# Gate stage: norm rows loaded step by step and transposes half a block later; the indexer's keys share two blocks of 328 columns with the values

## The chip, the cores and the metric

The kernel runs on one core of a Trainium2 chip. The metric is the device time of one execution in microseconds (us), the median of three runs. TensorE is called PE, VectorE DVE, ScalarE ACT, GpSimd POOL, and SyncE SP, as the profile does.

## The reference, cut to what matters

The program is a decoder trunk of two layers on 256 tokens of 2048 features, all in float32. The two stages that the change touches are the gated embedding at the end of each layer and the first half of the sparse-attention mixer of layer 1.

```
x = layer_norm(ALPHA * x + conv_glu(x)) * g + b
x = x + sigmoid(x @ ple_w_gate[i]) * (p[i] @ ple_w_proj[i])          # "gate stage"

q, k, v, qi, ki, wi = split(x @ dsa_w_in)      # 2048, 512, 512, 16*128, 128, 16 columns
ki = layer_norm(ki)                            # keys of the indexer
score[t, s] = sum_h wi[t, h] * relu(qi[t, h] . ki[s])    # 16 index heads
keep the 64 best s <= t for each t
o[h] = softmax(q[h] . k / sqrt(128) + bias[h, t - s]) @ v      # over the kept s, 16 heads
```

## The kernel before, in words

Every float32 weight is split into a high and a low part: a block of weights is loaded into a `raw` tile by a DMA that SP issues (L105), ACT writes `hi` (L109), DVE writes `lo` (L110), and PE multiplies both. `raw`, `hi` and `lo` have three buffers each, so a load can start when DVE has finished the `lo` of three blocks ago. Tokens are split likewise: `xT` holds the transposed x as a high and a low part.

There are two forms of matmul loop, both Python generators that hand over one step at a time. `gemm_t_steps` (L128, L132) holds the weights still and moves the tokens: 256 output columns at a time, 4 steps of 16 matmuls. `gemm_steps` (L154, L155, L158) holds the tokens still and moves n weight columns: per block of 128 features three matmuls for each half `a` of the tokens, so 96 matmuls over 16 blocks. With n = 512 a step covers 2 blocks of features (8 steps of 12 matmuls), with n = 144 it covers 4 (4 steps of 24). In the last step the two halves are finished one after the other, and `done(a, ps)` is called for each.

**Gate stage** (`ple`, both layers): four column blocks of 512. The first two run their first three steps by turns; then `affine` is called for four column slices: two row DMAs on POOL's queue (L205, one buffer each) and four DVE operations (L299, L300). Then the rest of the two blocks by turns, then blocks 2 and 3. `done` computes the sigmoid on ACT (L739), two DVE operations (L740, L741), and, in layer 0 only, transposes the new x with four PE transposes (`t_ps`, L199) into the `xT` of the next mixer (ACT L192, DVE L193).

**Sparse attention** (`dsa`, layer 1): the 144 columns of `ki` and `wi` run by turns with the first 256 columns of `qi`. `keys` normalizes each half with a chain of small DVE operations and transposes it on PE (`ki_ps`, L800). `index` computes one head's score (`sc_ps`, L813; ACT Relu L815; DVE L818 or L820). The other 14 heads follow (`scores`), and while the first eight are at hand POOL's queue gets eight loads of `bias` (L831). Then DVE finds the kept positions (L842, L843) and POOL adds the mask to `bias` (L848), while PE computes the keys `kT` and then the values `v` (512 columns). `attend` follows, two heads for every 256 columns of q: `lg_ps` L863, DVE L865 reads `bias`, and so on.

The order on each engine is fixed when the program is built: a scheduler takes the instructions in program order, moves an instruction ahead where it deems it ready earlier by its own estimates, and puts `hi` and `lo` 1000 places ahead (`W_AHEAD`). At run time each engine works through its list in order.

Of the kernel before, what the change touches and what calls it, by code (L numbers as in the profile page):

```python
# [16 lines left out]
P = 128  # L17
S = 256
D = 2048
KT = D // P  # L20
D_FF = 5120
ALPHA = 4.0 ** 0.25
LN_EPS = 1e-5
# [3 lines left out]
NR = 383  # L27
# [37 lines left out]
class Trunk:  # L65
# [30 lines left out]
                               reason="order")  # L96


    def weights(self, src, rows, nk, cols):

        nc = self.nc
        c0, n = cols
        shape = [P, nk, n]
        raw = self.wp.tile(shape, F32, tag="raw", name="raw")
        nc.sync.dma_start(out=raw, in_=src[rows:rows + nk * P, c0:c0 + n].rearrange("(k p) n -> p k n", p=P))  # L105
        hi = self.hl.tile(shape, F32R, tag="hi", name="hi")
        lo = self.hl.tile(shape, F32R, tag="lo", name="lo")
        with self.tc.high_priority(offset=W_AHEAD):
            nc.scalar.activation(hi, raw, AF.Copy)  # L109
            ins = nc.vector.tensor_tensor(lo, raw, hi.bitcast(F32), op=ALU.subtract)  # L110
        if self.behind:
            self.after(ins, self.behind.pop())
        return hi, lo
# [23 lines left out]
                done((c - c0 + o) // P, q[:m, :])  # L137
            yield

    def gemm_steps(self, src, c0, n, x, kt, done):  # L140


        nc = self.nc
        ps = [self.mm.tile([P, 512], F32, tag="mm", name="b_ps") for _ in range(2)]
        nk = min(1 << (1024 // n).bit_length() - 1, kt)
        for k0 in range(0, kt, nk):
            m = min(nk, kt - k0)
            hi, lo = self.weights(src, k0 * P, m, (c0, n))

            for halves in (range(2),) if k0 + m < kt else ((0,), (1,)):  # L150
                for k in range(m):
                    for a in halves:
                        xh, xl = (x(k0 + k)[:, j, a * P:(a + 1) * P] for j in range(2))
                        nc.tensor.matmul(ps[a][:, :n], xh, hi[:, k, :], start=k0 + k == 0, stop=False)  # L154
                        nc.tensor.matmul(ps[a][:, :n], xl, hi[:, k, :], start=False, stop=False)  # L155
                for k in range(m):
                    for a in halves:
                        self.last = nc.tensor.matmul(ps[a][:, :n], x(k0 + k)[:, 0, a * P:(a + 1) * P], lo[:, k, :],  # L158
                                                     start=False, stop=k0 + k == kt - 1)
                if k0 + m == kt:  # L160
                    done(a, ps[a][:, :n])
            yield
# [91 lines left out]
    def layer_norm(self, pool, st, g, b, gb, copies):  # L254


        nc, x, xT = self.nc, self.x, self.xT
        with self.tc.high_priority():
            mv = pool.tile([P, 2, 2], F32, tag="lmv", name="lmv")
# [35 lines left out]
        def affine(pool, nb, start):  # L295
            cs = slice(nb * 512, (nb + 1) * 512)
            gr, br = (self.rows(pool, r[cs], 512, k, 1, start) for r, k in ((g, "lng"), (b, "lnb")))
            for a in range(2):
                nc.vector.tensor_tensor(x[:, a, cs], x[:, a, cs], gr, op=ALU.mult)  # L299
                nc.vector.tensor_tensor(x[:, a, cs], x[:, a, cs], br, op=ALU.add)  # L300

        return affine

# [357 lines left out]
    def ffn(self, i, affine):  # L661
        nc, tc, t = self.nc, self.tc, self.t
        with tc.tile_pool(name="hp", bufs=1) as hp, tc.tile_pool(name="fp", bufs=1) as pool:
# [25 lines left out]
            for n in range(0, NF, 2):  # L689
                steps = (self.gemm_t_steps(t["ffn_w_gate"][i], n * P, 256, self.xT, lambda m, ps: gate(n + m, ps)),  # L690
                         self.gemm_t_steps(t["ffn_w_up"][i], n * P, 256, self.xT, lambda m, ps: up(n + m, ps)))
                if n:
                    for x in steps:
                        self.go_(x)
                else:
                    self.go_(*steps)
                if n % 4 == 0:
                    next(distances, None)
                if n in (6, 14, 22, 30):
                    affine(pool, n // 8, self.mark)  # L700
            return self.project(pool, t["ffn_w_down"][i], hT, NF, t["ln2_g"][i], t["ln2_b"][i], lambda: self.fill)


# [25 lines left out]
        return fill  # L729

    def ple(self, i, affine, xT=None, out=None):
        nc, tc, t, x = self.nc, self.tc, self.t, self.x
        with tc.tile_pool(name="pp", bufs=1) as pool:
            def done(nb):
                cs = slice(nb * 512, (nb + 1) * 512)

                def f(a, ps):
                    s = pool.tile([P, 512], F32, tag="sg", name="sg", bufs=2)
                    nc.scalar.activation(s, ps, AF.Sigmoid)  # L739
                    nc.vector.tensor_tensor(s, s, self.pw[:, a, cs], op=ALU.mult)  # L740
                    nc.vector.tensor_tensor(x[:, a, cs], x[:, a, cs], s, op=ALU.add)  # L741
                    if out is not None:
                        nc.sync.dma_start(out=out[0, a * P:(a + 1) * P, cs], in_=x[:, a, cs])
                    if xT is not None:
                        self.to_xT(xT, x[:, a, cs], a, nb * 4)
# [12 lines left out]


    def distances(self, pool):  # L760
# [21 lines left out]
    def dsa(self, pool, xT, oT):  # L782
        nc, tc, t = self.nc, self.tc, self.t
        w_in = t["dsa_w_in"]
        span = (P, S)
# [4 lines left out]
        ki = pool.tile([P, 2, P], F32, tag="ki", name="ki")  # L790
        pt = self.sp.tile([P, 2, P], F32, tag="sp", name="ki_ps")

        def keys(a, ps):
            nc.vector.tensor_scalar(wi[:, a], ps[:, P:], 1.0 / (4.0 * math.sqrt(128.0)), None, op0=ALU.mult)
            st = pool.tile([P, 6], F32, tag="kst", name="kst", bufs=2)
            nc.vector.bn_stats(st, ps[:, :P])
            mu, r = self.moments(pool, st, LN_EPS)
            nc.vector.scalar_tensor_tensor(ki[:, a], ps[:, :P], mu, g, op0=ALU.subtract, op1=ALU.mult)
            nc.vector.scalar_tensor_tensor(ki[:, a], ki[:, a], r, b, op0=ALU.mult, op1=ALU.add)
            nc.tensor.transpose(pt[:, a], ki[:, a], self.ident)  # L800
            if a:
                nc.vector.tensor_copy(kiT, pt.rearrange("p a s -> p (a s)"))


        sc = [pool.tile([P, span[a]], F32, tag=f"sc{a}", name=f"sc{a}") for a in range(2)]

        def index(h, ps):
            qi = pool.tile([P, S], F32, tag="qi", name="qi", bufs=2)
            self.fold(pool, qi, ps)
            p2 = self.sp.tile([P, 3 * P], F32, tag="sp", name="sc_ps")  # L810
# [4 lines left out]
            nc.scalar.activation(rl, p2, AF.Relu)  # L815
# [11 lines left out]
        def scores(n, ps):  # L827
            index(n + 2, ps)
            if n < 8:
                a, h = n // 4, n % 4 * 4  # L830
                nc.gpsimd.dma_start(out=bias[a][:, h:h + 4],  # L831
                                    in_=bass.AP(tensor=fx.tensor, offset=fx.offset + 255 - P * a + NR * h,
                                                ap=[[R, P], [NR, 4], [1, span[a]]]))

        self.gemm_t(w_in, 3328, 1792, xT, scores)

        for a in range(2):
# [48 lines left out]
    def run(self, out):  # L886
# [19 lines left out]
        self.ple(0, affine, xT=xT)  # L906
        pp.release()
        with tc.tile_pool(name="da", bufs=1) as pool:
            self.dsa(pool, xT, aT)
# [36 lines left out]
```

## Time and the profile before

| | us |
|---|---|
| median of three runs | 2877.74 |
| the three runs | 2878.88, 2877.74, 2874.36 |
| the profiled execution | 2870.2 |
| its span in the trace | 2868.4 |

The trace is that of the profiled execution, which was 7.5 us shorter than the median; 1.8 us of its time lie outside the span. All times of single instructions are on the span's clock. In the gate stage of layer 0 PE works from about 1611 to 1707 us, in the first half of the sparse attention from 1707 to 1873 us, and in the gate stage of layer 1 from about 2771 to 2863 us.

### The profile page before, as it was taken

What the parts mean: (1) busy time and instruction counts of PE and PEld (TensorE: products, weight loads), DVE (VectorE), ACT (ScalarE), POOL (GpSimd) and SP (SyncE); (2) the same over time, 40 slices, a digit from 0 to 9 for tenths busy, and PEclk for the clock granted to TensorE, in tenths of its full rate; (3) what the DMA queues carried; (4) which work ended last, traced back from release to release, by engine and by line L of the source; (5) the groups of instructions that cost most, each with busy time, mean ns of one, the idle gap of its engine ahead of it and who ended that gap; (6) DMA issues with size and microseconds to landing.
All of it is one profiled execution on the core that took longest, in us unless ns stands there. A gap on an engine that the chain in (4) does not pass through costs nothing.

```text
span 2868.4 us, 40302 instructions
## 1 busy us (share of the span) xinstructions
PE 2816.9 (98%) x15022; PEld 2406.3 (84%) x15022; DVE 1883.4 (66%) x3256; ACT 1401.6 (49%) x2147; POOL 311.8 (11%) x580
## 2 busy tenths in 40 slices
PE   8999999999999999999999999999999999999999
PEld 6788888888787888888888888888888888888887
DVE  6878877778655666666554755766576666654565
ACT  4455555555334655555433544455365555543354
POOL 0143234540000000000000000210000000000000
PEclk9999999999999999999999999999999999999999
DMA  6655556655465566666656566554656666656555
GB/s 195 174 154 152 162 158 164 173 151 144 140 221 176 185 201 202 200 204 205 194 194 192 191 190 182 173 157 138 195 167 196 194 191 197 198 191 191 191 190 191
DMA packets 409620, 520.90 MB, mean 182 GB/s; under 512 B 28268, under 2 KB 296944, under 8 KB 409168
## 3 DMA queue, kind: packets, MB, share of 16 engines
q1 hardware_dynamic: 402192, 499.91, 57.4%
q0 software_dynamic: 7232, 18.42, 2.6%
q8 instruction: 118, 1.93, 0.3%
q14 instruction: 78, 0.64, 0.1%
HBM read 514.00 MB, written 7.39 MB: 182 GB/s over the span
## 4 chain that ended last, share of the span: by engine, by line
PE 90%; DVE 5%; ACT 2%; DMA 2%; issue 1%; POOL 0%; SPq 0%; ACTq 0%; DVEq 0%; POOLq 0%
PE mm_ps L128 32%; PE mm_ps L132 16%; PE b_ps L158 12%; PE b_ps L155 11%; PE b_ps L154 11%; PE s_ps L526 2%; DVE lo L110 1%; ACT sqs L591 1%; PE w_ps L526 1%; ACT hi L109 1%; DMA raw<-in_gdn_w_in 1%; PE n_ps L283 1%; DVE ac L407 1%; PE o_ps L588 0%; PE g_ps L479 0%
## 5 line engine op out<-in xcount | busy, mean ns | idle before, releaser
L110 DVE TENSOR_TENSOR lo<-raw,hi 128x1024 fp32r<-128x1024 f32 x925 | 1135.4, 1228 | 805.1 <-ACT hi L109 771.9
L109 ACT ACTIVATE hi<-raw 128x1024 fp32r<-128x1024 f32 x925 | 977.5, 1057 | 1227.7 <-PE b_ps L155 499.9
L128 PE MATMUL mm_ps<-xT,hi 128*128 128x512 f32 x4176 | 1068.1, 396 | 1.1 <-DVE xT L193 1.1
L128 PEld LDWEIGHTS mm_ps<-xT,hi 128*128 128x128 f32 x4176 | 752.8, 190 | 135.7 <-DVE xT L193 1.7
L132 PEld LDWEIGHTS mm_ps<-xT,lo 128*128 128x128 f32 x4176 | 575.3, 190 | 40.9
L132 PE MATMUL mm_ps<-xT,lo 128*128 128x256 f32 x4176 | 602.8, 284 | 0.0
L154 PE MATMUL b_ps<-hi,xT 128*128 128x512 f32 (+1 forms) x704 | 272.3, 389 | 0.4 <-DVE xT L292 0.4
L155 PE MATMUL b_ps<-hi,xT 128*128 128x512 f32 (+1 forms) x704 | 272.5, 389 | 0.0
L154 PE MATMUL b_ps<-hi,hTA 128*128 128x512 f32 x512 | 199.4, 390 | 0.0
L155 PE MATMUL b_ps<-hi,hTA 128*128 128x512 f32 x512 | 199.2, 389 | 0.0
L158 PE MATMUL b_ps<-lo,xT 128*128 128x512 f32 (+1 forms) x704 | 197.1, 392 | 0.0
L155 PEld LDWEIGHTS b_ps<-hi,xT 128*128 128x128 f32 x704 | 133.6, 190 | 25.4 <-issue 0.4
L154 PEld LDWEIGHTS b_ps<-hi,xT 128*128 128x128 f32 x704 | 132.8, 189 | 26.1 <-DVE xT L292 0.7
L158 PEld LDWEIGHTS b_ps<-lo,xT 128*128 128x128 f32 x704 | 130.2, 190 | 25.1
L158 PE MATMUL b_ps<-lo,hTA 128*128 128x512 f32 x512 | 136.9, 389 | 0.0
L205 POOL DMA_DIRECT2D lng<-in_ln_g x16 | 8.7, 546 | 1123.8 <-DVE lo L110 556.4
L158 PEld LDWEIGHTS b_ps<-lo,hTA 128*128 128x128 f32 x512 | 96.1, 188 | 20.0
L155 PEld LDWEIGHTS b_ps<-hi,hTA 128*128 128x128 f32 x512 | 96.1, 188 | 19.9
L154 PEld LDWEIGHTS b_ps<-hi,hTA 128*128 128x128 f32 x512 | 96.1, 188 | 19.9
L154 PE MATMUL b_ps<-hi,oT 128*128 128x512 f32 x256 | 100.4, 392 | 0.3 <-DVE zs L556 0.3
L155 PE MATMUL b_ps<-hi,oT 128*128 128x512 f32 x256 | 100.2, 391 | 0.0
L512 POOL TENSOR_TENSOR xt<-ld,xi 128x60 f32<-128x60 f32 (+24 forms) x186 | 86.0, 462 | 69.3 <-DMA ld<-lt 55.2
(261 smaller groups left out, 2585.7 us busy)
## 6 DMA issues: line engine op xcount, KB each, us to landing
raw<-in_gdn_w_in SPq DMA_DIRECT2D x193, 512.0 KB, 3.9
raw<-in_ffn_w_gate SPq DMA_DIRECT2D x160, 512.0 KB, 3.9
raw<-in_ffn_w_up SPq DMA_DIRECT2D x160, 512.0 KB, 3.6
raw<-in_ffn_w_down SPq DMA_DIRECT2D x160, 512.0 KB, 3.7
raw<-in_dsa_w_in SPq DMA_DIRECT2D x80, 512.0 KB, 3.6
raw<-in_gdn_w_o SPq DMA_DIRECT2D x64, 512.0 KB, 3.7
raw<-in_ple_w_gate SPq DMA_DIRECT2D x64, 512.0 KB, 4.1
raw<-in_dsa_w_o SPq DMA_DIRECT2D x32, 512.0 KB, 3.8
```

What stands on the lines that cost most here:

```text
L109: nc.scalar.activation(hi, raw, AF.Copy)
L110: ins = nc.vector.tensor_tensor(lo, raw, hi.bitcast(F32), op=ALU.subtract)
L128: nc.tensor.matmul(q[:m, :], hi[:, k, o:o + m], x[:, k0 + k].rearrange("p a b -> p (a b)"), start=k0 + k == 0, stop=False)
L132: nc.tensor.matmul(q[:m, S:], lo[:, k, o:o + m], x[:, k0 + k, 0, :], start=False, stop=k0 + k == kt - 1)
L154: nc.tensor.matmul(ps[a][:, :n], xh, hi[:, k, :], start=k0 + k == 0, stop=False)
L155: nc.tensor.matmul(ps[a][:, :n], xl, hi[:, k, :], start=False, stop=False)
L158: self.last = nc.tensor.matmul(ps[a][:, :n], x(k0 + k)[:, 0, a * P:(a + 1) * P], lo[:, k, :], start=False, stop=k0 + k == kt - 1)
L283: ins = nc.tensor.transpose(ps[:, k, a * P:(a + 1) * P], x[:, a, (k0 + k) * P:(k0 + k + 1) * P], self.ident)
L407: nc.vector.scalar_tensor_tensor(ac, pd[:, k:k + S], w[:, k:k + 1], ac, op0=ALU.mult, op1=ALU.add)
L512: ins = eng.tensor_tensor(tmp[:, :m, :w], bcast(ld[:, i + 1:, i], m, 1), xi[:, :m, i:i + 1].to_broadcast([P, m, w]), op=ALU.mult)
L526: nc.tensor.matmul(ps[:, h], lhs[:, h], rhs[:, h], start=first, stop=last)
L591: nc.scalar.activation(sq, ps[:, h], AF.Square, accum_out=ss[:, a, h // 2, h % 2:h % 2 + 1])
```

## The change

- `weights` and `gemm_steps` take several column ranges: each gets its own DMA into one `raw` tile.
- In `ple` the first two blocks run six steps by turns; after each of the first four pairs one slice's two rows are loaded (four buffers each now, and the load waits for the last matmul of the pair), and the slice from two pairs before is applied. The two blocks are then finished one after the other. The transposes go into a list, and are called one after each step 1 to 6 of blocks 2 and 3; two are left over, and `dsa` calls them.
- In `dsa` the block of `ki` and `wi` also takes the first 184 columns of v, which makes 328; the other 328 columns of v are a second block (`rows`) right behind it. The v block between `kT` and `attend` is gone. `keys` first copies out of PSUM by ACT, normalizes both halves together, and its transposes come after six steps of `rows`. The scores of heads 0 and 1 come after that.
- Each `bias` load waits for the Relu of the latest score.

```diff
-    def weights(self, src, rows, nk, cols):
+    def weights(self, src, rows, nk, *cols):
...
+        for c0, n in cols:
+            nc.sync.dma_start(out=raw[:, :, o:o + n],
+                              in_=src[rows:rows + nk * P, c0:c0 + n].rearrange("(k p) n -> p k n", p=P))
+            o += n
...
     def ple(self, i, affine, xT=None, out=None):
...
                     if xT is not None:
-                        self.to_xT(xT, x[:, a, cs], a, nb * 4)
+                        rest.append(lambda: self.to_xT(xT, x[:, a, cs], a, nb * 4))
...
-            for _ in range(3):
+            loaded = []
+            for j in range(6):
                 for g in steps[:2]:
                     next(g)
-            for nb in range(4):
-                affine(pool, nb, None)
-            self.go_(*steps[:2])
-            self.go_(steps[2])
-            self.go_(steps[3])
+                if j < 4:
+                    loaded.append(affine(pool, j, self.last, 4))
+                if j >= 2:
+                    loaded.pop(0)()
+            self.go_(steps[0])
+            self.go_(steps[1])
+            for g in steps[2:]:
+                for j, _ in enumerate(g):
+                    if 0 < j < 7:
+                        turn()
+        return turn
...
+        NI, NV = P + 16, 184
+        def keys_values(a, ps):
+            nc.scalar.activation(ki[:, a], ps[:, :NI], AF.Copy)
+            nc.scalar.activation(v[:, a, :NV], ps[:, NI:], AF.Copy)
...
-        self.go_(self.gemm_steps(w_in, 5120, 144, lambda k: xT[:, k], KT, keys), self.gemm_t_steps(w_in, 3072, 256, xT, index))
+        steps = (self.gemm_steps(w_in, 5120, NI, lambda k: xT[:, k], KT, keys_values, ((2560, NV),)),
+                 self.gemm_t_steps(w_in, 3072, 256, xT, index))
+        next(steps[1])
+        for _ in range(2):
+            next(steps[0])
+            rest()
+        self.go_(*steps)
...
-                nc.gpsimd.dma_start(out=bias[a][:, h:h + 4],
+                ins = nc.gpsimd.dma_start(out=bias[a][:, h:h + 4],
...
+                self.after(ins, self.mark, sync=True)
...
+        rows = self.gemm_steps(w_in, 2560 + NV, 512 - NV, lambda k: xT[:, k], KT,
+                               lambda a, ps: nc.scalar.activation(v[:, a, NV:], ps, AF.Copy))
+        keys()
+        for _ in range(6):
+            next(rows)
+        turn()
+        for h in range(2):
+            score(h, first[h])
+        self.go_(rows)
         self.gemm_t(w_in, 3328, 1792, xT, scores)
...
-        v = pool.tile([P, 2, 512], F32, tag="vv", name="vv")
-        self.gemm(w_in, 2560, 512, lambda k: xT[:, k], KT, lambda a, ps: nc.scalar.activation(v[:, a], ps, AF.Copy))
+
```

## Rows read from the trace of the kernel before

**Rows 1.** The page: busy time of an engine, share of the span, instructions.

```profile
PE 2816.9 (98%) x15022; PEld 2406.3 (84%) x15022; DVE 1883.4 (66%) x3256; ACT 1401.6 (49%) x2147; POOL 311.8 (11%) x580
```

**Rows 2.** What PE waited for, whole span: us in total, times, longest.

```profile
PE t_ps L199 <- DVE x L741: 2.9, 3, 1.2
PE ki_ps L800 <- issue: 2.2, 1, 2.2
```

**Rows 3.** Stretches: length, busy time of each engine, granted clock, DMA share, GB/s.

```profile
1620.00:1658.00 38.00, 38.00 (x170) 31.46 (x169) 28.05 (x35) 17.56 (x20) 3.22 (x6) 1.00 0.68 218
...
1712.00:1715.00 3.00, 3.00 (x13) 2.81 (x13) 1.53 (x2) 1.29 (x2) 3.00 (x5) 0.50 0.60 82
...
1735.00:1738.00 3.00, 2.98 (x8) 2.42 (x9) 2.55 (x12) 0.00 (x0) 0.00 (x0) 0.50 0.28 63
2785.00:2860.00 75.00, 75.00 (x332) 62.11 (x331) 48.88 (x55) 32.28 (x34) 2.68 (x5) 1.00 0.66 215
```

**Rows 4.** Timeline of PE, gate's end and after: start, length, [idle before <- releaser].

```profile
1706.97 0.23 PE L154 MATMUL b_ps<-hi,xT 128*128 128x144 f32 x1
...
1710.74 0.86 PE L199 MATMUL t_ps<-ident,x 128*128 128x128 f32 x4 [1.14 <-DVE x L741]
...
1712.16 1.91 PE L158 MATMUL b_ps<-lo,xT 128*128 128x144 f32 x8
1713.87 3.71 PE L128 MATMUL mm_ps<-xT,hi 128*128 128x512 f32 x8
...
1718.53 0.23 PE L154 MATMUL b_ps<-hi,xT 128*128 128x144 f32 x1
```

**Rows 5.** Timeline of PE, the same loops at full clock, and the wait for the keys.

```profile
1724.01 0.23 PE L154 MATMUL b_ps<-hi,xT 128*128 128x144 f32 x1
...
1725.76 1.06 PE L158 MATMUL b_ps<-lo,xT 128*128 128x144 f32 x8
1726.65 2.05 PE L128 MATMUL mm_ps<-xT,hi 128*128 128x512 f32 x8
1728.55 1.11 PE L132 MATMUL mm_ps<-xT,lo 128*128 128x256 f32 x8
1729.49 0.23 PE L154 MATMUL b_ps<-hi,xT 128*128 128x144 f32 x1
...
1735.02 0.45 PE L800 MATMUL ki_ps<-ident,ki 128*128 128x128 f32 x1 [2.21 <-issue]
...
1738.99 1.32 PE L128 MATMUL mm_ps<-xT,hi 128*128 128x512 f32 x5
```

**Rows 6.** Timeline of PE, the block of v: its first matmul, and what follows it.

```profile
1851.57 0.40 PE L154 MATMUL b_ps<-hi,xT 128*128 128x512 f32 x1
...
1873.36 1.98 PE L128 MATMUL mm_ps<-xT,hi 128*128 128x512 f32 x8
```

**Rows 7.** Timeline of DVE: last gate operation, the first half's key chain, first bias read.

```profile
1709.91 0.68 DVE L741 TENSOR_TENSOR x<-x,sg 128x512 f32<-128x512 f32 x1
...
1731.39 0.17 DVE L794 TENSOR_SCALAR wi<-b_ps 128x16 f32<-128x16 f32 x1
...
1734.46 0.35 DVE L799 SCALAR_TENSOR_TENSOR ki<-ki,rs,kb 128x128 f32<-128x128 f32 x1
...
1887.48 0.62 DVE L865 SCALAR_TENSOR_TENSOR pr<-lg_ps,bias 128x128 f32<-128x128 f32 x2 [0.75 <-issue]
```

**Rows 8.** Timeline of POOL, 1700 to 2000 us: the second half's mask added to bias.

```profile
1858.10 18.18 POOL L848 TENSOR_TENSOR bias<-bias,sc 128x256 f32<-128x256 f32 x16 [3.01 <-DVE sc L846]
```

**Rows 9.** DMA issues of 1660 to 1706, then 1706 to 1735: KB each, us to landing.

```profile
raw<-in_dsa_w_in SPq DMA_DIRECT2D x3, 288.0 KB, 3.0
...
raw<-in_dsa_w_in SPq DMA_DIRECT2D x2, 288.0 KB, 5.7
```

**Rows 10.** Splits of 1700 to 1745 by shape: busy us, mean ns | idle before, releasers.

```profile
L110 DVE TENSOR_TENSOR lo<-raw,hi 128x576 fp32r<-128x576 f32 x4 | 3.0, 758 | 6.6 <-PE mm_ps L132 3.4 <-ACT hi L109 1.8 <-PE b_ps L158 1.4
L109 ACT ACTIVATE hi<-raw 128x576 fp32r<-128x576 f32 x4 | 2.7, 685 | 8.5 <-PE mm_ps L128 4.2 <-DMA raw<-in_dsa_w_in 2.3 <-PE b_ps L155 2.0
```

More of the change, by code (lines that the diff above doesn't have):

```diff
@@ L96, in after @@
                                reason="order")
-    def weights(self, src, rows, nk, cols):
+    def weights(self, src, rows, nk, *cols):
         nc = self.nc
-        c0, n = cols
-        shape = [P, nk, n]
+        shape = [P, nk, sum(n for _, n in cols)]
         raw = self.wp.tile(shape, F32, tag="raw", name="raw")
-        nc.sync.dma_start(out=raw, in_=src[rows:rows + nk * P, c0:c0 + n].rearrange("(k p) n -> p k n", p=P))
+        o = 0
+        for c0, n in cols:
+            nc.sync.dma_start(out=raw[:, :, o:o + n],
+                              in_=src[rows:rows + nk * P, c0:c0 + n].rearrange("(k p) n -> p k n", p=P))
+            o += n
         hi = self.hl.tile(shape, F32R, tag="hi", name="hi")
@@ L138, in gemm_t_steps, with gemm_steps @@
             yield
-    def gemm_steps(self, src, c0, n, x, kt, done):
+    def gemm_steps(self, src, c0, n, x, kt, done, also=()):
         nc = self.nc
+        cols = ((c0, n), *also)
+        n = sum(m for _, m in cols)
         ps = [self.mm.tile([P, 512], F32, tag="mm", name="b_ps") for _ in range(2)]
@@ L147, in gemm_steps @@
             m = min(nk, kt - k0)
-            hi, lo = self.weights(src, k0 * P, m, (c0, n))
+            hi, lo = self.weights(src, k0 * P, m, *cols)
             for halves in (range(2),) if k0 + m < kt else ((0,), (1,)):
@@ L293, in layer_norm, with affine, apply @@
                 nc.vector.tensor_tensor(lo, xb, hi.bitcast(F32), op=ALU.subtract)
-        def affine(pool, nb, start):
+        def affine(pool, nb, start, bufs=1):
             cs = slice(nb * 512, (nb + 1) * 512)
[L297 to L300, printed above, removed]
+            gr, br = (self.rows(pool, r[cs], 512, k, bufs, start) for r, k in ((g, "lng"), (b, "lnb")))
+            def apply():
+                for a in range(2):
+                    nc.vector.tensor_tensor(x[:, a, cs], x[:, a, cs], gr, op=ALU.mult)
+                    nc.vector.tensor_tensor(x[:, a, cs], x[:, a, cs], br, op=ALU.add)
+            return apply
         return affine
@@ L699, in ffn @@
                 if n in (6, 14, 22, 30):
-                    affine(pool, n // 8, self.mark)
+                    affine(pool, n // 8, self.mark)()
             return self.project(pool, t["ffn_w_down"][i], hT, NF, t["ln2_g"][i], t["ln2_b"][i], lambda: self.fill)
@@ L732, in ple, with turn @@
         nc, tc, t, x = self.nc, self.tc, self.t, self.x
+        rest = []
+        def turn():
+            if rest:
+                rest.pop(0)()
         with tc.tile_pool(name="pp", bufs=1) as pool:
@@ L780, in distances, with dsa @@
             self.after(ins, self.mark, sync=True)
-    def dsa(self, pool, xT, oT):
+    def dsa(self, pool, xT, oT, rest):
         nc, tc, t = self.nc, self.tc, self.t
@@ L789, in dsa @@
         kiT = pool.tile([P, S], F32, tag="kiT", name="kiT")
[L790 to L802, printed above, removed]
+        ki = pool.tile([P, 2, P + 16], F32, tag="ki", name="ki")
@@ new lines, in dsa, with keys @@
+        v = pool.tile([P, 2, 512], F32, tag="vv", name="vv")
+        NI, NV = P + 16, 184
+        def keys_values(a, ps):
+            nc.scalar.activation(ki[:, a], ps[:, :NI], AF.Copy)
+            nc.scalar.activation(v[:, a, :NV], ps[:, NI:], AF.Copy)
+        def keys():
+            mv = pool.tile([P, 2, 2], F32, tag="kmv", name="kmv")
+            z = pool.tile([P, 2], F32, tag="kz", name="kz")
+            for a in range(2):
+                st = pool.tile([P, 6], F32, tag="kst", name="kst", bufs=2)
+                nc.vector.bn_stats(st, ki[:, a, :P])
+                nc.vector.bn_aggr(mv[:, a], st)
+            nc.vector.tensor_scalar(z, mv[:, :, 1], LN_EPS, None, op0=ALU.add)
+            r = self.rsqrt(pool, z, 2)
+            for a in range(2):
+                y = ki[:, a, :P]
+                nc.vector.scalar_tensor_tensor(y, y, mv[:, a, 0:1], g, op0=ALU.subtract, op1=ALU.mult)
+                nc.vector.scalar_tensor_tensor(y, y, r[:, a:a + 1], b, op0=ALU.mult, op1=ALU.add)
+            nc.vector.tensor_scalar(wi, ki[:, :, P:], 1.0 / (4.0 * math.sqrt(128.0)), None, op0=ALU.mult)
@@ L805, in dsa, with turn @@
+        def turn():
+            pt = self.sp.tile([P, 2, P], F32, tag="sp", name="ki_ps")
+            for a in range(2):
+                nc.tensor.transpose(pt[:, a], ki[:, a, :P], self.ident)
+            nc.vector.tensor_copy(kiT, pt.rearrange("p a s -> p (a s)"))
         sc = [pool.tile([P, span[a]], F32, tag=f"sc{a}", name=f"sc{a}") for a in range(2)]
+        first = []
         def index(h, ps):
@@ L809, in index, with score @@
             self.fold(pool, qi, ps)
+            if h > 1:
+                score(h, qi)
+            else:
+                first.append(qi)
+        def score(h, qi):
             p2 = self.sp.tile([P, 3 * P], F32, tag="sp", name="sc_ps")
@@ L814, in index @@
             rl = pool.tile([P, 3 * P], F32, tag="rl", name="rl", bufs=2)
-            nc.scalar.activation(rl, p2, AF.Relu)
+            self.mark = nc.scalar.activation(rl, p2, AF.Relu)
             for a, r in enumerate((rl[:, 0:P], rl[:, P:])):
@@ L830, in scores @@
                 a, h = n // 4, n % 4 * 4
-                nc.gpsimd.dma_start(out=bias[a][:, h:h + 4],
-                                    in_=bass.AP(tensor=fx.tensor, offset=fx.offset + 255 - P * a + NR * h,
-                                                ap=[[R, P], [NR, 4], [1, span[a]]]))
+                ins = nc.gpsimd.dma_start(out=bias[a][:, h:h + 4],
+                                          in_=bass.AP(tensor=fx.tensor, offset=fx.offset + 255 - P * a + NR * h,
+                                                      ap=[[R, P], [NR, 4], [1, span[a]]]))
+                self.after(ins, self.mark, sync=True)
[8 more added lines that the diff above has]
+        self.go_(rows)
         self.gemm_t(w_in, 3328, 1792, xT, scores)
@@ L905, in run @@
         xT, aT = big[:, :16], big[:, 16:]
-        self.ple(0, affine, xT=xT)
+        rest = self.ple(0, affine, xT=xT)
         pp.release()
         with tc.tile_pool(name="da", bufs=1) as pool:
-            self.dsa(pool, xT, aT)
+            self.dsa(pool, xT, aT, rest)
         pp = tc.alloc_tile_pool(name="pw1", bufs=1, side="right")
```

## The prediction

> **What bounds the kernel.** I read the page first. PE is busy for 2816.9 of 2868.4 us [rows 1], so some 51 us of idle PE are all that waiting can give back in the whole kernel. A change can gain in three ways: fewer PE microseconds, less PE idle time, or less PE time at a low clock. Everything that merely lightens DVE, ACT or the queues is worth nothing by itself. The second view was the list of what PE waited for. Two of its entries lie in changed code: the gate's transposes waited 2.9 us for DVE in three places, and the transpose of the indexer's keys waited 2.2 us [rows 2]. Third, the stretches with their granted clock. In the gate stage of layer 0 PE is busy for 38.00 of 38.00 us until the first transpose, and in that of layer 1 for 75.00 of 75.00 us [rows 3]; there nothing can be won. Behind the gate of layer 0 the granted clock is 0.50 in two stretches, the lower of the two levels, 1.2 of 2.4 GHz [rows 3]. Fourth, the timeline of PE there. Each low stretch follows idle time: of 1.14 us before a transpose (with another wait shortly before it), and of 2.21 us before the key transpose [rows 4, 5]. So the place to price is from 1658 to 1740 us, and then the block of v that moves.
>
> **Rows step by step in the gate stage.** The same 8 row loads and 16 DVE operations remain in each layer; they only come later and with four buffers. They cost PE nothing now, and DVE is busy for 28.05 of 38.00 us [rows 3], so I cost this at 0. What hides it is the 43 us that two gate blocks take (2 x 21.8, below). A pair of steps is 2 x 2.72 = 5.4 us, (a step is 21.8 / 8 us) and a row is used two pairs after its load was released. Without that cover a late slice would delay the sigmoid sum of its block and with it the transposes. The row loads now wait for PE on POOL's queue; behind them stand only the two loads for the key norm, wanted 100 us later. That layer 1 gains or loses nothing follows from its full PE.
>
> **Transposes half a block later.** No PE instruction is added or removed: eight groups of four before and after. What goes are the three waits, 2.9 us [rows 2], and the low clock behind them. That is worked out by comparing the same groups at both clocks. The eight `lo` matmuls of 144 columns took 1713.87 - 1712.16 = 1.71 us at the low clock [rows 4] and 1726.65 - 1725.76 = 0.89 us at full clock [rows 5]: 0.8 lost. The step of 16 took 1718.53 - 1713.87 = 4.66 us [rows 4] against 1729.49 - 1726.65 = 2.84 us [rows 5]: 1.8 lost. Together 2.6 us; some 0.5 us in the few instructions just before is not counted. What is late next? The last gate operation on DVE ended at 1709.91 + 0.68 = 1710.6 us [rows 7], 3.6 us after the gate's last matmul at 1707.0 [rows 4]. In the new order one index step (2.84 us) and two shared steps (1.8 us each, below) stand ahead of the last group, 6.4 us. That leaves 2.8 us. In blocks 2 and 3 each group has at least two steps of 2.72 us ahead of it. If the cover were gone the 2.9 us would come back. The index step and the shared steps read the late part of `xT` (features 12 to 15) only in the fourth and the seventh step.
>
> **The keys with the values.** Before, 96 matmuls of 144 columns: a step of 24 took 1726.65 - 1724.01 = 2.64 us [rows 5], 0.110 each, so 10.6 us in all; and 96 of 512 columns took 1873.36 - 1851.57 = 21.8 us [rows 6], 0.227 each. Together 32.4 us. After, 192 of 328 columns, a length that the trace lacks. The nearest rows: 256 columns take (1729.49 - 1728.55) / 8 = 0.118 us [rows 5], 512 take 0.227. From below, 192 x 0.118 = 22.6, a gain of 9.8; from above, 192 x 0.227 = 43.6, a loss of 11.2. Between 256 and 512 the price grows by 0.43 ns a column, and 144 columns cost nearly what 256 do: a floor per matmul, and above it a price per column. On that line 328 columns take 0.148 us, 28.5 us in all: 3.9 us gained. A step is 12 x 0.148 = 1.78 us.
>
> The Trainium skill (TensorE: Matmul & The Clock Gate, Back-to-back issue gap) gives N / 2.4 + 2.5 ns for one matmul at full clock, 139 ns for 328 columns. By that the 192 would take 26.7 us, the gain would be 5.7 and the sum below 14.9; its 216 ns for 512 columns is less than the 227 of the row, so I keep the line through the rows.
>
> **The key chain.** PE waited 2.21 us for it and then ran at the low clock: from 1735.02 to 1738.99 are 3.97 us [rows 5] for one transpose, six `hi` and eight `lo` matmuls, which at full clock take 2.84 - 2 x 0.24 + 0.1 = 2.5 us; 1.5 lost, with the clock at 0.50 [rows 3]. In total 3.7 us go. The chain itself took 1734.81 - 1731.39 = 3.4 us for one half [rows 7]. The new one does both halves with one root: I estimate 5 us, plus 0.4 for the ACT copy and four `lo` of 0.86 between, 9 us. Six steps of `rows` cover 6 x 1.78 = 10.7 us. So no wait, with 1.7 us to spare; what exceeds it would be paid on PE, though two more steps of `rows` (3.6 us) are there to fill it.
>
> **The bias loads, and v gone from behind kT.** The loads now wait for a Relu each; nothing is queued behind them on POOL until the mask is added over 100 us later. Cost 0. But the mask loses cover: 21.8 us of PE work between `kT` and `attend` move ahead of the search for the kept positions. The first read of `bias` moves from 1887.5 [rows 7] to 1865.7 on the same clock. The second half's additions start at 1858.1 and take 18.18 / 16 = 1.14 us a head [rows 8], so head 0 is ready at 1859.2, 6.5 us early, and each further head costs POOL 1.14 us where PE takes two index steps, 5.7 us. Cost 0.
>
> **Sum.** -2.9 (waits) - 2.6 (low clock behind them) - 3.9 (columns) - 2.2 - 1.5 (key chain) = -13.1 us. Against the profiled execution, 2870.2 us, that is 2857.1. That execution was 7.5 us below the median of the three, so on the median's footing 2877.7 - 13.1 = 2864.6 us, -0.46%.
>
> **Rivals.**
>
> *Weights come late to the short steps.* Three key-value steps run without an index step between, then eight of `rows`: 11 steps of 1.78 us with 328 KB each. A `raw` buffer is taken for load, `hi` and `lo`. By the 288 KB loads that is 3.0 us without company [rows 9], scaled to 3.1, and by the splits of 576 columns 0.69 and 0.76 us [rows 10], scaled by 656 / 576 to 0.78 and 0.86; with 0.5 for hand-overs (an estimate) 5.2 us, over three buffers 1.75 a step. PE takes 1.78: just covered. With the 5.7 us that such loads took beside the bias loads [rows 9] it is 7.84 / 3 = 2.6, 0.8 more a step, 9 us in all: 2874, no difference. For it: no slack in the plain case. Against it: the bias loads now come later, and six buffers of weights are filled ahead. A landing of 4.2 us would cost 3.6 us: 2868.
>
> A rule of the Trainium skill speaks for this rival (DMA: Bandwidth & Descriptors, Bandwidth): loads should be batched to 1 MiB or more, since small ones pay a fixed cost; here 12 loads become 24 smaller ones. No row shows whether a third load in flight would hide it.
>
> *The same with the clock.* Idle spells of 0.8 us in every step could bring the clock down for the whole stretch, as 1.14 and 2.21 us did before [rows 4, 5]. At the lower level 11 steps take 19.6 us more: 2884, slower. It decides only if loads land at 5 us or more throughout.
>
> *Waits only move.* The list of PE is fixed when the program is built, by estimates, and before they put the key transpose 2.2 us too early. If they again put it, or the gate's groups, ahead of their data, up to 9.2 us come back: 2874 with both, about 2869 with one.
>
> *The first bias read waits for all additions.* If DVE waited for the whole tile, POOL's end at 1876.3 [rows 8] would be 10.6 us late, with some low clock behind it: 2877, no difference.
>
> **How the numbers follow.** The forecast as it stands, 2864.6 (its own range 2859 to 2869, from the columns between 26.7 and 30 us and the spread of the runs): 0.66. Still faster but less: weights somewhat late (2868) 0.09, one wait back (2869) 0.08. No difference: weights late by 0.8 us a step 0.05, both waits back 0.03, the bias read 0.03. Slower, by the clock: 0.06. About 0.2%, 5.8 us, is what a measurement of this kernel can tell from no change. So faster 0.83, same 0.11, slower 0.06. The range to 8 in 10 goes from 2857 (a price near the 256-column bound) to 2873.
>
> **What would show it.** Right: no `t_ps` or `ki_ps` among PE's waits, a granted clock of 1.00 from the gate's end to the scores, matmuls of 328 columns some 0.148 us apart, the stretch from 1707 to `attend` shorter by some 12 us, and the gate of layer 1 as long as before. Wrong: starts of the 328-column matmuls over 0.2 us apart, ACT's `hi` waiting for DMA in `rows` with PE idle, a `tp_ps` wait right after `kT`, or a clock of 0.50 anywhere in the stretch.

## The result, and the profile after

The changed kernel takes 2856.74 us (median of 6 runs, 2854.44 to 2861.07), the kernel before 2873.50 on the same chips: ratio 0.9946, interval 0.9934 to 0.9957, so faster by 0.54% against the 0.46% forecast. On the median that the prediction started from, 2877.74, the ratio gives 2862.2. As it stands 2856.74 lies just below the stated range of 2857 to 2873: the three runs that the forecast started from were slower than the later ones, so its base was too high by some 4 us. The profiled executions have spans of 2855.6 and 2868.4 us: 12.8 less, where the sum said 13.1.

The page of the changed kernel, and what PE waited for in changed code (us in total, times, longest); they answer to [rows 1] and [rows 2]:

```profile
PE 2807.7 (98%) x15022; PEld 2400.8 (84%) x15022; DVE 1883.0 (66%) x3246; ACT 1403.0 (49%) x2155; POOL 312.7 (11%) x580
...
PE b_ps L159 <- ACT hi L112: 1.2, 2, 0.6
...
PE tp_ps L940 <- DVE pr L937: 0.9, 3, 0.4
```

`t_ps` behind the gate and `ki_ps` are gone from the list. In their place stand two waits of 0.6 us, one in each gate stage, and 0.9 us at the start of `attend`. The stretches that answer to [rows 3] (busy time of PE, PEld, DVE, ACT, POOL, then the granted clock, DMA share, GB/s):

```profile
1620.00:1658.00 38.00, 37.42 (x165) 30.64 (x164) 28.52 (x36) 18.09 (x21) 4.28 (x8) 1.00 0.71 231
1707.00:1712.00 5.00, 5.00 (x38) 4.98 (x37) 3.51 (x5) 2.88 (x4) 1.06 (x2) 1.00 0.56 114
1712.00:1730.00 18.00, 18.00 (x115) 17.04 (x114) 9.05 (x12) 8.10 (x12) 0.00 (x0) 1.00 0.63 184
1730.00:1742.00 12.00, 12.00 (x82) 12.00 (x81) 9.59 (x29) 5.47 (x11) 0.00 (x0) 1.00 0.67 190
```

From the gate's end to the key transposes PE does not stop and the clock is 1.00 throughout. PE's timeline there answers to [rows 4, 5]:

```profile
1705.10 1.98 PE L131 MATMUL mm_ps<-xT,hi 128*128 128x512 f32 x8
...
1709.68 0.60 PE L204 MATMUL t_ps<-ident,x 128*128 128x128 f32 x4
...
1711.92 0.60 PE L204 MATMUL t_ps<-ident,x 128*128 128x128 f32 x4
...
1731.50 0.31 PE L159 MATMUL b_ps<-hi,xT 128*128 128x328 f32 x1
...
1733.30 0.32 PE L159 MATMUL b_ps<-hi,xT 128*128 128x328 f32 x1
...
1742.32 0.38 PE L843 MATMUL ki_ps<-ident,ki 128*128 128x128 f32 x2
```

A step of 12 matmuls of 328 columns takes 1.80 us, 0.150 each. I cut the kernel into three parts at points that both traces have: **A** from the first transpose of layer 0's gate stage (1607.97, before 1607.83) to the gate's last matmul; **B** from there (1705.10, before 1706.97) to the first matmul of q for `attend` (1858.95, before 1873.36); **C** from there to the end. All work ahead of A is the same, yet A started anywhere from 1604.8 to 1615.6 us in the executions profiled here. This noise lies outside the change, so the parts tell the kernels apart better than the totals do. Each is from a single execution all the same: the kernel before, profiled twice, has B at 166.4 and 167.0, and the changed gate stage, which seven of the runs below share, has A at 97.0 to 98.7.

| us | A | B | C | PE busy in B | idle in B |
|---|---|---|---|---|---|
| before | 99.1 | 166.4 | 995.0 | 162.4 | 3.9 |
| changed | 97.1 | 153.9 | 996.7 | 153.7 | 0.2 |

So B gives 12.5 us, of which 3.7 are idle time and 8.8 PE time; A gives 2.0, of which about half belongs to the execution (last section), and C takes 1.6 back.

### The profile page after: what moved, and what is told of

It is laid out like the page before. It is cut to its first block, busy times and chain, and to the rows that moved or that the text cites. A ratio compares the mean times of both kernels' runs of the same rounds, so it can differ in the third digit from the quotient of the medians.

```text
span 2855.6 us, 40342 instructions
## 1 busy us (share of the span) xinstructions
PE 2807.7 (98%) x15022; PEld 2400.8 (84%) x15022; DVE 1883.0 (66%) x3246; ACT 1403.0 (49%) x2155; POOL 312.7 (11%) x580
## 5 line engine op out<-in xcount | busy, mean ns | idle before, releaser
L113 DVE TENSOR_TENSOR lo<-raw,hi 128x1024 fp32r<-128x1024 f32 (+1 forms) x929 | 1133.9, 1222 | 799.3 <-ACT hi L112 772.0
L112 ACT ACTIVATE hi<-raw 128x1024 fp32r<-128x1024 f32 (+1 forms) x929 | 978.2, 1053 | 1216.2 <-PE b_ps L160 480.2
```

## The experiments

Part times are single profiled executions; ratios are against the kernel before on the same chip, from four to twelve runs of each experiment.

**The gate stage alone** (`e1_gate_only`), and **the attention part alone** (`e2_attention_only`):

```diff
 e1: the changed kernel, with dsa of before, but in place of one go_ over its two loops
+        next(steps[1])
+        for _ in range(2):
+            next(steps[0])
+            rest()
+        self.go_(*steps)
 e2: the changed kernel, with ple of before
```

> The gate stage as changed (rows step by step, transposes half a block later), the indexer's keys and the values as before. Three stretches of the trace are compared: A from the first norm transpose of layer 0's gate stage to its last matmul (before 99.1 us, changed 97.1), B from there to the first matmul of q (before 166.4, changed 153.9), C from there to the end (before 995.0, changed 996.6). My theory: the waits and the clock are separate local costs that add up, so A is 97.1, B loses only the transposes' waits and low clock (1.7 + 2.6 + 0.5 us), 161.6, and the key wait of 2.2 us is still there; C loses only the half microsecond of layer 1's gate stage, 995.6. In all some -6 us, ratio 0.998. Rival: the clock is what matters and the key wait alone keeps it low, so B stays above 164 and the whole is within 3 us of before.

> The gate stage as before, keys and values as changed. My theory: A stays at 99.1 us, B keeps the transposes' waits and the low clock behind them (4.8 us) and loses 3.6 us by the columns and 3.7 by the keys, so 159; C is 996 because the new waits in the attention (0.9 us) come from the values' block being gone in front of it. In all some -6.5 us, ratio 0.998. Rival: the gains do not add, B is 154 already, because the index block no longer starts behind the transposes.

e1: ratio 0.9985 (0.9976 to 0.9994), B 166.6 where 161.6 was expected: nothing gained in B. e2: 0.9961 (0.9946 to 0.9975), B 153.9, as its rival had it: everything gained in B, with the old gate stage. In e1 the transposes no longer wait, and PE's timeline shows where their gain went:

```profile
1735.54 0.45 PE L825 MATMUL ki_ps<-ident,ki 128*128 128x128 f32 x1 [7.07 <-issue]
```

The key wait grew from 2.2 to 7.1 us. The timelines of ACT and then DVE say why. The weights of the key block (128x576) were there, and PE had finished the first half of the keys at 1726.6 us. But in DVE's list a `lo` of the `qi` weights (128x1024) stands ahead of the key chain (L819 and after), and the `hi` that it needs stood for its load. The chain began 5.3 us late.

```profile
1729.67 1.06 ACT L112 ACTIVATE hi<-raw 128x1024 fp32r<-128x1024 f32 x1 [6.98 <-DMA raw<-in_dsa_w_in]
```

```profile
1730.76 1.23 DVE L113 TENSOR_TENSOR lo<-raw,hi 128x1024 fp32r<-128x1024 f32 x1 [6.81 <-ACT hi L112]
1731.90 0.17 DVE L819 TENSOR_SCALAR wi<-b_ps 128x16 f32<-128x16 f32 x1
```

In e1's DMA issues of 1708 to 1735 (KB each, us to landing) the `bias` loads stand beside it:

```profile
raw<-in_dsa_w_in SPq DMA_DIRECT2D x6, 512.0 KB, 4.9
bias<-fx POOLq DMA_DIRECT2D x4, 512.0 KB, 9.8
bias<-fx POOLq DMA_DIRECT2D x4, 256.0 KB, 6.3
```

That is 3 MB at some 340 GB/s (the GB/s of e1's stretches there are 324 and 348), about 9 us of all 16 DMA engines, in the place where PE and the key chain need weights. Hence the next experiments.

**The bias loads' wait**: taken out of the changed kernel (`e8_bias_free`), put alone into the kernel before (`e10_before_bias_wait`), and put into e1 (`e11_gate_bias_wait`):

```diff
+            self.mark = nc.scalar.activation(rl, p2, AF.Relu)
...
+                self.after(ins, self.mark, sync=True)
```

> As changed, but the eight bias loads do not wait for a score and start as soon as POOL reaches them, as before, beside the weights of the shared blocks. My theory: they start near the end of the gate, about 3.3 MB in 10 us, weight loads beside them land in 5 to 8 us and not 3 to 3.6, but the stretch alternates short and long steps there and weights are three blocks ahead, so PE waits at most 2 us in all, B is 153.9 to 156. Rival: with steps of 1.8 us the late loads stop PE for 0.8 us a step, and with the clock falling B is 160 or more.

> The kernel before, with one part of the change alone: each of the eight bias loads waits for the Relu of the latest score. Theory 1: beside the bias loads the weights arrived late (5.7 us to land), DVE's list held the key chain behind such a late split, and that was part of the key wait; without it the wait falls from 2.2 to about 1.5 us and B from 166.4 to 165. Theory 2: the chain of 3.4 us alone sets it and nothing changes. Theory 3: the bias loads were the whole reason, the wait goes, and B is below 163.

> The gate stage as changed and the attention as before, as in the first experiment, but each bias load waits for a score. There PE waited 7.1 us for the keys, and ACT's hi had waited 7.0 us for a weight load. Theory 1: the bias loads did it, since the gate's end came earlier relative to them; without them beside the weights the key wait falls back to some 2 us, and B from 166.6 to the 161.6 us that I had expected there. Theory 2: the order of the steps did it (an index step first, so the keys end before their chain can), the wait stays above 5 us and B above 165.

e8: 0.9981 (0.9969 to 0.9992), B 159.8 where at most 156 was expected, so 5.9 us of the gain are lost without the wait. PE then waited for ACT's `hi`; 3.0 and 1.4 us of these waits lie in B, the rest in the gate stages:

```profile
PE b_ps L159 <- ACT hi L112: 4.6, 3, 3.0
PE mm_ps L131 <- ACT hi L112: 1.4, 1, 1.4
```

e10: 0.9978 (0.9968 to 0.9989), B 163.3 with a key wait of 1.83 us, between its theories: 3.0 us gained by that wait alone. e11: 0.9971 (0.9959 to 0.9984), B 160.1, 6.5 us less than e1, and its key wait is 1.82 us, so the order of the steps was not the reason. The ratios of e1 and e11 do not tell the two apart, since their intervals overlap; the parts do. The bias loads were thus a cause of the lost time in B, which the prediction priced at 0.

**The kernel before, profiled once more** (`e12_before_again`), unchanged:

> The kernel before, unchanged, profiled once more. With the wait for a score added to its bias loads alone, the low clock behind the transposes and behind the key transpose was gone although PE still waited 0.58, 1.14 and 1.83 us there. Theory: the low clock is this kernel's own, since the bias loads stand beside those waits; then it is there again, the granted clock 0.50 in two stretches between 1710 and 1742 us, and the stretch from the gate's end to the first matmul of q is 166 us again. Rival: which idle spell is followed by the lower level differs from one execution to the next; then one or both low stretches are missing, and the stretch is 1.5 to 4 us shorter, 162.5 to 165. The waits themselves (0.6, 1.1 and 2.2 us) are the same by both.

Neither held. PE's timeline, then three stretches (columns as above):

```profile
1707.32 0.63 PE L199 MATMUL t_ps<-ident,x 128*128 128x128 f32 x4 [1.14 <-DVE x L741]
...
1732.46 0.45 PE L800 MATMUL ki_ps<-ident,ki 128*128 128x128 f32 x1 [6.28 <-issue]
```

```profile
1709.00:1712.00 3.00, 3.00 (x21) 2.67 (x19) 1.53 (x2) 1.21 (x2) 3.00 (x5) 1.00 0.85 135
1712.00:1715.00 3.00, 3.00 (x27) 2.96 (x26) 0.81 (x2) 1.06 (x1) 2.80 (x4) 1.00 1.03 302
...
1732.00:1735.00 3.00, 2.54 (x7) 2.09 (x8) 2.83 (x12) 0.00 (x0) 0.00 (x0) 0.50 0.14 27
```

The same 1.14 us wait was this time not followed by the low clock, but the key wait was 6.3 us instead of 2.2, and B took 167.0 us against 166.4. DVE began the key chain 25.3 us after the gate's last matmul, against 24.4 the first time (1731.39 [rows 7] less 1706.97) and 20.8 in e10, where the bias loads came later. PE had finished the first half of the keys 4.5 us before that here, and 0.4 us before it the first time. So the first low stretch had cost PE time that it would otherwise have spent waiting for the same loads. All of B in one row each (length, busy time of PE first, granted clock third from the end), in turn e12, e10, e11 and the changed kernel.

```profile
1703.56:1870.59 167.03, 159.03 (x907) 138.47 (x906) 102.98 (x203) 68.74 (x93) 32.86 (x40) 0.98 0.59 181
```

```profile
1706.81:1870.14 163.33, 159.27 (x907) 138.89 (x906) 103.00 (x203) 69.01 (x93) 32.90 (x40) 0.99 0.61 185
```

```profile
1703.79:1863.91 160.12, 157.58 (x907) 137.57 (x906) 103.36 (x203) 69.05 (x93) 32.89 (x40) 1.00 0.62 190
```

```profile
1705.10:1858.95 153.85, 153.66 (x907) 137.76 (x906) 96.30 (x179) 70.93 (x100) 14.13 (x21) 1.00 0.66 197
```

By the first two the bias loads' wait took away 3.9 us of idle time (8.0 to 4.1). Against the first execution of the kernel before, which was idle for 3.9, it took away 3.2 us of PE time at the low clock instead (162.4 to 159.3).

The last two hold the same number of matmuls at full clock. They differ by 157.58 - 153.66 = 3.9 us of PE time, which is the columns, and by 2.5 - 0.2 = 2.3 us of idle time, which is the key chain and a short wait behind it.

**The columns back at 144 and 512** (`e3_144_and_512`), with four steps of `rows` ahead of the key transposes:

```diff
-        NI, NV = P + 16, 184
+        NI, NV = P + 16, 0
```

> As changed, but the columns are not shared: the keys keep a block of 144 columns and the values one of 512, right behind it, so order and cover stay those of the change. My theory: only the column price comes back, 96 x 0.110 + 96 x 0.227 = 32.4 us against 192 x 0.150 = 28.8 us, so B is 157.5 us and nothing waits. Rival: the shared blocks are worth nothing by themselves and B stays within 1 us of 153.9, all of the gain being waits and clock.

0.9963 (0.9949 to 0.9978), B 157.2, all of it busy at full clock: 3.4 us more, the price of the columns by another pair.

**Fewer steps ahead of the key transposes** (`e6_keys_after_two`: two instead of six), and **the last block's transposes called at once** (`e5_last_transposes_at_once`):

```diff
-        for _ in range(6):
+        for _ in range(2):
             next(rows)
...
-                        rest.append(lambda: self.to_xT(xT, x[:, a, cs], a, nb * 4))
+                        if nb == 3:
+                            self.to_xT(xT, x[:, a, cs], a, nb * 4)
+                        else:
+                            rest.append(lambda: self.to_xT(xT, x[:, a, cs], a, nb * 4))
```

> As changed, but the key transposes and the first two scores stand after two steps of the second value block and not after six. In the changed kernel the key chain on DVE ends 6.5 us after the key block's last matmul, and two steps cover 3.6 us. My theory: PE waits about 2 to 3 us for the keys again, with some low clock behind it, B is 156 to 158 us. Rival: the order on PE is fixed by estimates good enough to put more value steps ahead, and B stays at 153.9.

> As changed, but the two groups of transposes of the gate's last block are put where they were before, right behind it; the other six stay half a block later. My theory: two waits of 0.6 and 1.1 us come back, and with them the low clock (3 us), so stretch B (gate's last matmul to the first matmul of q) grows from 153.9 to some 158.5 us. Rival: idle time costs only itself and the low clock before had another cause (the bias loads that ran at the same time), so B grows by 1.7 us and the granted clock stays at 1.00.

e6: 0.9958 (0.9943 to 0.9973), B 154.3, a key wait of 0.5 us, so its rival held. e5: 0.9965 (0.9953 to 0.9976), B 154.2, no `t_ps` wait, so neither of its two held. In both the scheduler placed other ready steps ahead of the transposes by itself. By these runs the written order is hardly needed, as long as there is independent work at hand.

**The rows all at once again** (`e4_rows_at_once`):

```diff
-                if j < 4:
-                    loaded.append(affine(pool, j, self.last, 4))
-                if j >= 2:
-                    loaded.pop(0)()
+                if j == 2:
+                    for nb in range(4):
+                        affine(pool, nb, None)()
```

> As changed, but the norm rows are loaded and applied as before, all four slices after three pairs of steps, one buffer. My theory: the rows step by step are worth nothing and cost a little. In the changed kernel DVE stands 4.1 us still for a row load with weight splits queued behind it, ACT waits 5.7 us, and PE waits 0.6 us in each gate stage. Without it those two waits go, A is 96.5 us and C 0.6 us shorter, -1.2 us in all against the changed kernel. Rival: the rows step by step are what keeps the clock up at the start of the gate stage (granted clock 0.70 there before, 1.00 now), and A grows by 1 us or more.

0.9951 (0.9934 to 0.9968). Its part A is 96.25 us, 0.9 less than in the changed kernel, and the two waits for `hi` are gone. In the changed kernel they come from a row that is late. DVE's timeline, then ACT's:

```profile
1629.34 0.69 DVE L307 TENSOR_TENSOR x<-x,lng 128x512 f32<-128x512 f32 x1 [4.11 <-issue]
```

```profile
1631.23 1.06 ACT L112 ACTIVATE hi<-raw 128x1024 fp32r<-128x1024 f32 x1 [5.65 <-DVE lo L113]
```

DVE stood 4.1 us for the row, the `lo` queued behind it freed its buffers late, and at 1639.6 us PE waited 0.58 us for a `hi`.

**Loads half as large** in the two 328-column blocks (`e7_half_loads`: one block of 128 features each, 164 KB):

```diff
-        nk = min(1 << (1024 // n).bit_length() - 1, kt)
+        nk = nk or min(1 << (1024 // n).bit_length() - 1, kt)      # nk = 1 for both blocks
```

> As changed, but the two blocks of 328 columns load one block of 128 features at a time: 164 KB where it was 328, twice as many loads, the same matmuls. It tests the rival by which the weights come late to the short steps. A load of 144 KB took 2.3 us to land in the changed kernel and one of 184 KB 3.7 us; with hi (about 0.4), lo (0.45) and 0.5 for hand-overs a buffer turns in 3.6 to 5 us, over three buffers 1.2 to 1.7 us a half step, where PE takes 0.9. My theory: now the loads do bind: PE idles some 0.3 to 0.8 us in each of 22 half steps, B grows by 7 us or more, with the clock falling. Rival: loads overlap well enough even so, and B stays within 2 us of 153.9; then the loads were never near binding.

1.0012 (1.0000 to 1.0024), B 167.9: 14.1 us more, which is more than the whole gain of B. PE's waits in B make 7.0 us of it; the other 7 are busy time (160.7 against 153.7), some of it at a granted clock of 0.83 between 1715 and 1725 us:

```profile
PE mm_ps L131 <- ACT hi L112: 4.5, 3, 2.3
PE b_ps L159 <- ACT hi L112: 2.5, 4, 1.0
```

The edit also halves what the three buffers hold ahead and doubles the number of splits, so this run does not show which of the three, the size of a load, the depth or the splits, brought the waits.

**Half of `kT` as the cover, rows at once, `rows` ahead of `attend`** (`e9_keys_half_as_cover`): e4's gate stage; three steps of the first half of `kT` stand ahead of the key transposes, and the second block of v follows `kT`, so the mask's additions have more PE work beside them.

```diff
         keys()
-        for _ in range(6):
-            next(rows)
+        half = self.gemm_t_steps(w_in, 2048, 256, xT, lambda n, ps: self.fold(pool, kT[:, n], ps))
+        for _ in range(3):
+            next(half)
         turn()
...
+        self.gemm_t(w_in, 2304, 256, xT, lambda n, ps: self.fold(pool, kT[:, n + 2], ps))
+        self.go_(rows)
```

> As changed, with the norm rows at once as before, and with other cover: the first half of kT runs behind the shared key block and covers the key chain, the second block of the values runs between the second half of kT and attend. No work is added or left out. My theory: the gate stages gain what the rows at once gave (A 96.3 us, layer 1's gate stage 93.6), and the three waits of 0.9 us at the start of attend go, since PE does 11.2 + 14.4 us and not 22.4 between the last score and attend; B is 153.9, all in all 3 us less than the changed kernel in the three stretches. Rival: those waits come from POOL and DVE working side by side and stay wherever attend begins, or the key chain is not covered by 8.5 us of kT and PE waits 1 to 3 us.

0.9951 (0.9937 to 0.9966), so no measurable difference from the changed kernel (0.9946). B is 153.4 us. C is 994.8, 1.8 less than in the changed kernel, but that is layer 1's gate stage: 93.7 against 95.9 us, 0.6 of it the `hi` wait and 1.7 PE time, the granted clock of its first 12 us being 1.00 against 0.86. PE's waits for `pr` fell from 0.9 to 0.4 us, and a wait of 0.4 for `qq` came. A is 97.8, not the 96.3 expected, with a granted clock of 0.86 in its first 12 us. So of the 3 us expected 1.6 came, and the clock hides what the other cover is worth.

## Why the prediction was right, and where its steps were not

**The sum.** 13.1 us forecast, 12.8 in the spans: right in size, put together partly from wrong terms. That the two agree so closely is luck: a term priced at 0 gave 3.0 us, two others gave 2.5 less than forecast, and C took 1.6 back. The chain before → e10 → e11 → changed splits B by what was altered. The split holds for this order of steps only; e2 has the whole gain of B without the new gate stage.

| us | measured | forecast |
|---|---|---|
| bias loads wait (166.4 → 163.3) | 3.0 | 0 |
| gate's last transposes behind other steps (→ 160.1) | 3.2 | 4.3 (1.7 waits, 2.6 clock) |
| key chain covered (idle 2.5 → 0.2) | 2.3 | 3.7 (2.2 wait, 1.5 clock) |
| columns (157.6 → 153.7) | 3.9 (3.4 by e3) | 3.9 |

Of the second row, 1.5 us are waits and 1.7 PE time at the low clock, which in e10 lay behind the key wait and in e11 was missing; that share may belong to the execution.

**Columns: right.** 0.150 us a matmul against 0.148 by the line through [rows 5, 6], and the gain is the forecast's. The Trainium skill (TensorE: Matmul & The Clock Gate, Back-to-back issue gap) gave 139 ns and a gain of 5.7; the measured 150 ns decides for the line.

**"The low clock behind them", 2.6 us: the step that failed.** In [rows 3, 4] the low stretch was real, but it was priced as if PE would save it. In e12 it did not occur, and the key wait took 4.1 us more; e1 took the transposes' waits away altogether, and the key wait was 7.1 us. As long as the bias loads delayed weights whose `lo` stands ahead of the key chain on DVE, neither could be saved. I read the waits one by one and did not ask what the last of them depended on: ACT was waiting for loads there before, too (2.3 us in [rows 10]).

**"The bias loads: cost 0": the step that hid it.** The text looked at what is queued behind the loads on POOL and not at what they take from the loads on SP, though [rows 9] had 288 KB in 5.7 us beside them and 3.0 alone. Moving them is worth 3.0 us alone, 6.5 on top of the new gate stage (e1 to e11), and 5.9 in the finished kernel (e8). It is not an extra beside the other parts: the key wait could not go without it.

**The gate's deferral** was credited with the transposes' waits. Of these only the one inside A needs it: e2 has the old gate stage, B as short as the changed kernel, and one `t_ps` wait of 1.6 us in A. There, as in e5, both last groups stand behind matmuls of the index step, which the new attention part begins with.

**Key chain: right, with more slack.** It ended about 6.5 us after the key block's last step (1731.5 to 1738.0 on DVE), not 9, under a cover of 10.8. The transposes at 1742.3 did not wait. DVE's timeline:

```profile
1737.40 0.61 DVE L837 SCALAR_TENSOR_TENSOR ki<-ki,rs,kb 128x128 f32<-128x128 f32 x2
```

**Rows step by step: 0 was too low** by 0.6 us of wait a stage. The cover was counted in PE time up to the transposes; the late row held up the `lo` of other weights, behind it in DVE's list. That its load had not landed is inferred: the profile names no releaser, and the four loads of `lng` took 4.9 to 7.7 us to land.

**v gone from behind kT: not quite 0.** A `tp_ps` wait was among the prediction's signs of being wrong, and 0.9 us of it came. The first bias read comes early and by parts, as argued (rival 4 did not come): it is released at 1873.4 while POOL adds until 1881.5. But DVE is slowed beside POOL. The changed kernel's POOL and DVE timelines; before, the same two `pr` operations took 0.55 us at 1890.91, with POOL done:

```profile
1865.47 16.03 POOL L915 TENSOR_TENSOR bias<-bias,sc 128x256 f32<-128x256 f32 x16 [3.01 <-DVE sc L913]
```

```profile
1873.39 0.62 DVE L931 SCALAR_TENSOR_TENSOR pr<-lg_ps,bias 128x128 f32<-128x128 f32 x2 [0.75 <-POOL bias L915]
1873.93 0.60 DVE L933 TENSOR_REDUCE sm<-pr 128x1 f32<-128x128 f32 x2
...
1877.05 1.50 DVE L937 TENSOR_SCALAR pr<-pr,sm 128x128 f32<-128x128 f32 x2
1878.48 1.75 DVE L113 TENSOR_TENSOR lo<-raw,hi 128x1024 fp32r<-128x1024 f32 x1
```

The scaling took 0.95 us more and the `lo` 0.5 more, while the reduction and the read from PSUM kept their times. Together with a `hi` wait of 0.6 in layer 1 the `tp_ps` wait of 0.9 is most of C's 1.6. The Trainium skill (SBUF — State Buffer, Who interferes with whom) states this split: a scaling out of and into SBUF, or an operation with two inputs there, can be blocked by GpSimd for a whole instruction, a reduction never. The rows agree.

**Weights late to the short steps: did not come, but was close.** No wait for `hi` lies in the eleven steps; the median landings are well below the 5 us at which the rival decides. The rival's sum was also off in one place: 3.0 us for 288 KB, scaled by size, is 3.4 for 328 KB, not 3.1. With the 3.6 that came its rule gives 1.9 us a step where PE takes 1.8, and still no wait: the rule was too strict. DMA issues of 1700 to 1748:

```profile
raw<-in_dsa_w_in SPq DMA_DIRECT2D x8, 328.0 KB, 3.6
raw<-in_dsa_w_in SPq DMA_DIRECT2D x6, 184.0 KB, 3.7
raw<-in_dsa_w_in SPq DMA_DIRECT2D x6, 144.0 KB, 2.3
```

With bias loads beside them (e8) or at half the size (e7) it comes. The Trainium skill's advice to batch loads (DMA: Bandwidth & Descriptors, Bandwidth) is in line with e7, where size, depth and splits changed together; from 512 to 328 KB the trace shows no wait.

**Layer 1's gate stage** was forecast unchanged: 95.9 us against 95.0 before (95.2 in e12), all three with a granted clock of 0.86 in the first 12 us; 0.6 of it is the `hi` wait.

## What to carry to other kernels

Two waits in a row are not two gains: ask of the last one what it depends on, and whether time saved ahead of it only makes it longer. A profile of the same kernel from a second execution shows such a trade for nothing. When large loads are moved, price them by what they take from the other queues' loads in the old place and in the new, before counting the instructions around them.

## What the runs showed of the hardware that was not expected

The low clock does not follow from the length of one idle spell. Behind the same 1.14 us the granted clock fell to 0.50 in one of three executions of this order (before; not in e12 or e10); behind a key wait of 1.83 us it fell in e10, behind one of 1.82 in e11 it stayed at 1.00. In the norm that opens the gate stage 12 transposes took 2.82 us before and 1.58 in e12 (PE's timelines), behind the same waits, the longest of 1.09 us:

```profile
1612.09 2.82 PE L283 MATMUL n_ps<-ident,x 128*128 128x128 f32 x12 [0.27 <-ACT x L273]
```

```profile
1609.59 1.58 PE L283 MATMUL n_ps<-ident,x 128*128 128x128 f32 x12 [0.26 <-ACT x L273]
```

What decides it stays open. At the same point of the changed kernel they took 1.58, so about 1 us of A's gain of 2.0 is owed to the execution: against e12 A gives 1.1, B 13.2, and C takes 1.5, 12.7 in all.

This sorts A in all 14 profiles. Its first 12 us have a granted clock of 0.86 in five (before, e1, e3, e6, e9) and of 1.00 in nine. At 1.00 A is 98.2 to 98.5 us with the gate stage of before, 97.0 to 98.0 with the changed one and 96.25 with the rows at once (e4); at 0.86 it is 99.1, 98.5 to 98.7 and 97.8 (e9). So the changed gate stage gains some 0.5 to 1 us in A, and the rows at once another 0.7 or more, by single executions.
